# Weight sums for half of the up projection made in DRAM instead of on VectorE, in one paced list, with w_up laid out by blocks

## The chip, the cores and the metric

The kernel is one program on 1 core of one Trainium2 chip. The metric is the device time of one execution in microseconds, as the median of three runs. The profile is of one execution, read by a hardware profiler; its span is the time from the first to the last instruction that it shows.

## What is computed

One decoder layer on a sequence of 512 tokens of width 1024, in float32. An input projection feeds four token mixers of 4 heads each, their normed outputs go through one output projection, and a squared-ReLU MLP of width 4096 follows. The change touches the MLP and the weight loads around it:

```python
mixed = jnp.concatenate([rms_norm(gr, group_out_g[i]) for i, gr in enumerate(groups)], axis=-1)
x = x + mixed @ w_o
u = jax.nn.relu(rms_norm(x, mlp_norm_g) @ w_up)      # 1024 -> 4096
return x + (u * u) @ w_down                           # 4096 -> 1024
```

## The kernel before

**Split arithmetic.** TensorE works on fp32r operands. Each float32 operand is split into a rounded high part and a remainder, and a product is three matmuls, high x high, high x low, low x high (`mm3`). A weight block of 128x512 is loaded from DRAM into a raw room (tile `wraw`), ScalarE makes the high part (`whi<-wraw`), VectorE subtracts it to make the low part (`wlo<-wraw,whi`), and the pair waits in a pool of `WB` = 10 pairs until TensorE has used it.

**Fewer products.** Up and down projection use a Strassen-Winograd scheme: 7 products of half-size blocks in place of 8, paid for with sums of weight blocks and of activations. The up projection runs over 8 feature groups G of 512 columns and two halves c of the contraction. In a group, products 1, 2, 5, 6, 7, 3, 4 come in this order for c = 0 and then for c = 1; one product of one c is 12 matmuls of 128x256. Products 1, 2 and 4 use a raw block of weights. Products 5, 6, 7 and 3 use weight sums: VectorE makes them from the raw rooms, one `TENSOR_TENSOR` of 128x512 each, into tiles named `pT` and `sq` (`pair_load`, `split_st`): 4 sums for each (G, c), 64 in all. The accumulators of a group lie in banks named `ps_s`, `ps_o`, `ps_t` and `ps_acc`, two of each; `combine_first` and `combine` add them up on VectorE and ScalarE and so free them.

**Early products.** For the groups in `EARLY` = 1, 3, 5, 7, products 1 and 2 run ahead of group 0, during the norm of the residual stream (`first_products`). They need a bank of `ps_o` each.

**Rooms and loads.** There are three raw rooms of 128x1024. `pair_load` gets two of them for each (G, c) and fills each with one 512 KB transfer. The down projection uses the same rooms as six halves, plus `pT`, `pT`, `sq` once the up stage no longer needs them. Its own weight sums (products 5, 6, 7 for 8 pairs of blocks, 24 sums) are not made on VectorE: SyncE starts a DRAM-to-DRAM copy of 512 KB into a tile `wsum`, and GpSimd starts an accumulating DMA (`dma_add`) that adds the second block; `weight_sums(G)` ties each to the start of an attention unit or to the end of a product of the up stage.

**Order.** The program is written by a planner: generators for each piece of work (`pl.spawn(..., priority)`) are stepped against modelled engine clocks; `Get` and `pl.put` hand buffers round, `Wait` waits for named events. What it settles is only the order of instructions on each engine. On the chip each engine runs its list in order, and semaphores for data and buffers decide when. A transfer that waits for a room on SyncE therefore holds every later transfer of SyncE's list.

**Names in the profile.** `act` is L293, `tt` (a VectorE or GpSimd tensor_tensor) L301, `mm3`'s matmul L321, transposes L333, `dma` L338, `dma_add` L343. In the changed file the same helpers stand 11 lines further down.

## Time and profile before

| | us |
|---|---|
| median of 3 runs (606.76, 608.39, 612.29) | 608.39 |
| the profiled execution's own time | 607.45 |
| its span | 605.3 |

The profiled execution is 0.94 us under the median, and 2.15 us of its time lie outside the span. The up stage begins about 300 us after the span's start with group 0, the down projection's first matmuls are at about 450 us, and the last output is stored at the end of the span. A busy share is read with its stage: TensorE is busy in nearly all of the span, so time can be gained only where it waits or where its clock is low.

### The profile page before, as it was taken

To read this page: it belongs to the slowest core of one execution; us is meant where nothing else is said; L and a number is where in the kernel's file an instruction comes from. 1 tells how busy PE (TensorE), PEld (TensorE's weight loads), DVE (VectorE), ACT (ScalarE), POOL (GpSimd) and SP (SyncE) were. 2 spreads that over 40 slices of the span, in tenths; PEclk is the share of its full clock that TensorE was granted. 3 is DMA by queue.
4 is the path that set the end of the run, shared out by engine and by line. 5 is a ranking of instruction groups with operands and counts; after the bars stand their busy time and mean duration, and the time that the engine had idled before them with its cause. 6 is when DMAs were issued, how large, how long until landed. Compare 5 with 4: busy or idle time off the path is not lost.

```text
span 605.3 us, 10541 instructions
## 1 busy us (share of the span) xinstructions
PE 585.5 (97%) x3556; PEld 515.6 (85%) x3556; DVE 492.6 (81%) x1141; ACT 385.0 (64%) x877; POOL 102.3 (17%) x153
## 2 busy tenths in 40 slices
PE   8999998999999999999989999999979999999997
PEld 7978887887899878889989999999968888888885
DVE  4775669589978796669899999998989999989652
ACT  6766566467766675558657577566676766766640
POOL 5134453462312110000000000000011111100000
PEclk9999999999999999999989999999998999999999
DMA  6953905299986240404347767656598778656622
GB/s 196 291 161 93 317 10 140 43 196 309 322 141 106 35 140 1 140 11 130 105 139 201 197 180 198 189 184 182 142 301 218 188 192 200 169 179 220 192 85 104
DMA packets 54118, 99.06 MB, mean 164 GB/s; under 512 B 5238, under 2 KB 12976, under 8 KB 53936
## 3 DMA queue, kind: packets, MB, share of 16 engines
q1 hardware_dynamic: 44592, 81.42, 41.6%
q0 software_dynamic: 9312, 16.83, 17.1%
q8 instruction: 28, 0.46, 0.3%
q14 instruction: 26, 0.21, 0.1%
q10 hardware_dynamic: 160, 0.14, 0.1%
HBM read 96.27 MB, written 27.26 MB: 204 GB/s over the span
## 4 chain that ended last, share of the span: by engine, by line
PE 69%; DVE 13%; DMA 9%; ACT 5%; issue 3%; SPq 0%; DVEq 0%; ACTq 0%
PE ps_acc L321 21%; PE ps_o L321 17%; PE ps_t L321 14%; PE ps_s L321 13%; PE ps_t L333 4%; DMA wraw<-in_w_up_dram 3%; DMA wraw<-in_w_o_dram 3%; ACT whi L293 2%; DMA wraw<-in_w_in_dram 2%; DVE wlo L305 1%; DVE p L301 1%; DVE wlo L301 1%; DMA wraw<-wsum 1%; DVE q L305 1%; DMA rnb<-in_x_dram 1%
## 5 line engine op out<-in xcount | busy, mean ns | idle before, releaser
L321 PE MATMUL ps_acc<-whi,xT 128*128 128x512 f32 (+1 forms) x416 | 144.3, 403 | 0.8 <-ACT kT L293 0.4
L321 PEld LDWEIGHTS ps_acc<-whi,xT 128*128 128x128 f32 x416 | 77.7, 190 | 12.1 <-ACT kT L293 0.8
L321 PE MATMUL ps_acc<-wlo,xT 128*128 128x512 f32 (+1 forms) x208 | 83.3, 405 | 0.0
L293 ACT ACTIVATE whi<-wraw 128x512 fp32r<-128x512 f32 x95 | 59.0, 625 | 29.1 <-DMA wraw<-in_w_up_dram 6.6
L301 DVE TENSOR_TENSOR wlo<-wraw,whi 128x512 fp32r<-128x512 f32 x95 | 64.5, 686 | 10.7 <-ACT whi L293 10.4
L343 POOL DMA_DIRECT2D wsum<-in_w_down_dram x24 | 22.1, 1054 | 210.8 <-DMA wsum<-in_w_down_dram 209.2
L293 ACT ACTIVATE whi<-pT 128x512 fp32r<-128x512 f32 x57 | 35.7, 628 | 26.4 <-DVE pT L301 16.8
L293 ACT ACTIVATE p<-p,sm 128x256 f32<-128x256 f32 (+3 forms) x64 | 34.4, 539 | 18.1 <-DVE sm L1013 17.8
L321 PEld LDWEIGHTS ps_acc<-wlo,xT 128*128 128x128 f32 x208 | 39.6, 190 | 5.5
L321 PE MATMUL ps_s<-kT,q 128*128 128x256 f32 (+3 forms) x150 | 42.7, 334 | 1.5 <-DVE sm L1013 0.8
L301 DVE TENSOR_TENSOR wlo<-pT,whi 128x512 fp32r<-128x512 f32 x57 | 38.8, 686 | 3.4 <-ACT whi L293 3.3
L305 DVE SCALAR_TENSOR_TENSOR wlo<-wraw,ga_col,whi 128x512 fp32r<-128x512 f32 (+1 forms) x40 | 31.6, 803 | 10.4 <-ACT whi L293 10.1
L321 PE MATMUL ps_o<-kT,whi 128*128 128x256 f32 (+1 forms) x204 | 39.7, 289 | 0.0
L321 PEld LDWEIGHTS ps_o<-kT,whi 128*128 128x128 f32 x204 | 32.3, 190 | 0.6
L321 PEld LDWEIGHTS ps_s<-kT,q 128*128 128x128 f32 x150 | 26.8, 190 | 5.5 <-DVE sm L1013 2.4
L293 ACT ACTIVATE whi<-wraw,ga_col 128x512 fp32r<-128x512 f32 (+1 forms) x40 | 27.1, 700 | 5.0 <-DMA wraw<-in_w_in_dram 4.7
L321 PE MATMUL ps_o<-kT,wlo 128*128 128x256 f32 (+1 forms) x102 | 29.5, 290 | 0.6 <-DVE wlo L301 0.6
L321 PE MATMUL ps_o<-q,whi 128*128 128x256 f32 (+1 forms) x136 | 26.5, 292 | 2.6 <-ACT whi L293 2.5
L301 POOL TENSOR_TENSOR rnb<-rnb,sm 128x512 f32<-128x512 f32 (+3 forms) x20 | 18.0, 904 | 65.3 <-DVE sm L301 24.9
L333 PE MATMUL ps_t<-ident,p 128*128 128x128 f32 x148 | 26.7, 274 | 0.3 <-ACT p L293 0.3
L293 ACT ACTIVATE whi<-sq 128x512 fp32r<-128x512 f32 x28 | 17.5, 626 | 13.3 <-DVE sq L301 7.9
L321 PEld LDWEIGHTS ps_o<-q,whi 128*128 128x128 f32 x136 | 21.4, 191 | 3.5 <-issue 2.4
(542 smaller groups left out, 1736.8 us busy)
## 6 DMA issues: line engine op xcount, KB each, us to landing
wraw<-in_w_up_dram SPq DMA_DIRECT2D x32, 512.0 KB, 3.8
wsum<-in_w_down_dram POOLq DMA_DIRECT2D x24, 512.0 KB, 7.5
wraw<-wsum SPq DMA_DIRECT2D x36, 256.0 KB, 3.0
wsum<-in_w_down_dram SPq DMA_DIRECT2D x16, 512.0 KB, 6.7
wraw<-in_w_down_dram SPq DMA_DIRECT2D x32, 256.0 KB, 3.4
wraw<-in_w_in_dram SPq DMA_DIRECT2D x24, 256.0 KB, 3.1
wraw<-in_w_o_dram SPq DMA_DIRECT2D x16, 256.0 KB, 4.0
wsum<-wsum SPq DMA_DIRECT2D x8, 512.0 KB, 7.8
```

Of the source, the lines that this page charges most:

```text
L293: lambda: nc.scalar.activation(o, i, func, scale=scale, **kw), aps(o, accum), aps(i, scale, bias))
L301: lambda: E[eng].tensor_tensor(o, a, b, op=op), [o], [a, b])
L305: lambda: nc.vector.scalar_tensor_tensor(o, a, s, b, op0=op0, op1=op1), [o], aps(a, s, b))
L321: nc.tensor.matmul(o, l, r, start=first, stop=last)
L333: nc.tensor.transpose(o, i, ident[0:parts, 0:parts])
L343: return Op("pool", 1000.0 * nb / 262144, lambda: nc.gpsimd.dma_start(out=o, in_=i, accum_op=ALU.add), [o], [o], nb, 2100.0)
```

## The change

Five edits:

1. **Up sums in DRAM.** For groups 1, 3, 5 and 7 (`UPSUMS`) the four weight sums are made in DRAM (tiles `wsumu`), each by a copy on SyncE and an accumulating DMA on GpSimd, 16 of each. These groups then load five 256 KB blocks for each c, two to a room, in place of two 512 KB transfers. 32 VectorE sums go. Since a DMA only adds, the signs of three products are turned and three additions in `combine` become subtractions.
2. **One list of sums.** All 40 sums (16 up, then 24 down) stand in one list. Number n is released by the planner at 115,000 + 7,500 n ns of its TensorE clock, its add 8,000 ns later. On the chip this sets only the places of the copies in SyncE's list and of the adds in GpSimd's.
3. **Rows of the adds.** `dma_add` now cuts the rows of a transfer at 512 bytes (`max_dma_last_dim=512`; 128 elements), and the planner counts an add's bytes twice.
4. **w_up by blocks.** On the host, w_up is laid out so that each block of 128x512 is contiguous; the early loads read rows of 2 KB, not 1 KB.
5. **Rooms singly, four early banks.** `up_rooms` hands a room to the up stage as soon as both its halves are back, not all three at once; groups 3 and 7 take the `ps_acc` banks for their early products.

```diff
+UPSUMS = (1, 3, 5, 7)
+SUM_AT, SUM_NS, SUM_LAG = 115000.0, 7500.0, 8000.0
...
     def dma_add(o, i):
         nb = n_of(o) * o.shape[0] * 4
-        return Op("pool", 1000.0 * nb / 262144, lambda: nc.gpsimd.dma_start(out=o, in_=i, accum_op=ALU.add), [o], [o],
-                  nb, 2100.0)
+        return Op("pool", 1000.0 * nb / 262144, lambda: nc.gpsimd.dma_start(out=o, in_=i, accum_op=ALU.add,
+                                                                              max_dma_last_dim=512), [o], [o],
+                  2.0 * nb, 2100.0)
...
+    USUM = {(pr, G): dram.tile([2 * P, 512], F32, name=f"wsumu{pr}{G}", tag=f"wsumu{pr}{G}")
+            for G in UPSUMS for pr in (5, 6, 7, 3)}
...
-                k0 = (4 * j + 2 * c) * P
-                LOADS.append((("st", G, c, 1 + j), [(w_up[0, k0:k0 + 2 * P, G * 512:G * 512 + 256].rearrange(
-                    "(k p) f -> p k f", p=P), 512)], None, 1, None))
+                LOADS.append((("st", G, c, 1 + j), [(w_up[G, 0, j, c], 512)], None, 1, None))
...
             if q[0][0] == ("st", 0, 0):
-                for _ in range(2 * WRAW):
-                    yield Get("wraw")
-                for room in RAW2:
-                    pl.put("wraw2", room)
+                pl.spawn(up_rooms(), 1)
...
+        if G in UPSUMS:
+            srcs = {1: w_up[G, 0, 0, c], 2: w_up[G, 0, 1, c], 4: w_up[G, 1, 1, c]}
+            for j in range(0, len(todo), 2):
+                room = yield Get("wraw2")
+                left = [room, len(todo[j:j + 2])]
+                for n, pr in enumerate(todo[j:j + 2]):
+                    raw = room[:, n * 512:(n + 1) * 512]
+                    if pr not in srcs:
+                        yield Wait(("sum", pr, "up", G))
+                    yield dma(raw, srcs[pr] if pr in srcs else USUM[pr, G][c * P:(c + 1) * P])
+                    pl.spawn(split_sum(key(pr), raw, left, turn[pr]), split_prio)
+            return
...
+    def split_sum(key, raw, left, turn):
+        yield Wait(("turn", turn))
+        hi, lo = yield Get("w")
+        pl.events.add(("turn", turn + 1))
+        yield from split(hi, lo, raw)
+        left[1] -= 1
+        if not left[1]:
+            pl.put("wraw2", left[0])
...
     def first_products(G):
-        banks = {}
+        banks, tag = {}, ("o", "acc")[EARLY.index(G) % 2]
         for pr in (1, 2):
-            banks[pr] = yield Get("o")
+            banks[pr] = yield Get(tag)
...
-    def weight_sums(G):
-        for pr, ev, src in ((5, (G, 12 + G), rows(1, 1, G * 4, 2)), (6, (24 + 3 * G, 30 + 3 * G), rows(2, 2, G * 4 + 2, 2)),
-                            (7, (5, 3), rows(2, 2, G * 4 + 2, 2))):
...
+    def weight_sums():
+        for n, (where, pr, G, first, second) in enumerate(sum_list()):
+            dst = (USUM if where == "up" else WSUM)[pr, G]
+            yield At(SUM_AT + n * SUM_NS)
+            yield dma(dst, first)
+            pl.spawn(weight_add(SUM_AT + n * SUM_NS + SUM_LAG, where, pr, G, dst, second), 2)
+
+    def weight_add(at, where, pr, G, dst, src):
+        yield At(at)
+        yield dma_add(dst, src)
+        pl.events.add(("sum", pr, where, G))
```

TensorE's list is the same for the first 517 of some 2,720 entries, holds the same work in another order through the attention, and is the same again from group 0 of the up stage to the end. VectorE's list falls from 1118 to 1084 entries, SyncE's grows from 220 to 259, GpSimd's from 145 to 160.

VectorE at group 0, before. `pT` and `sq` hold weight sums of group 0, `whi` and `wlo` are split weights, and `xT<-ps_o_65` is `combine_first` of group 7, which frees the second bank of `ps_o`:

```order
L301 TENSOR_TENSOR pT_147<-wraw_107,sq_146 128x512
L301 TENSOR_TENSOR wlo_120<-sq_146,whi_119 128x512
L301 TENSOR_TENSOR wlo_126<-wraw_107,whi_125 128x512
L301 TENSOR_TENSOR wlo_124<-pT_147,whi_123 128x512
L301 TENSOR_TENSOR xT_2851<-ps_o_65,xT_2851 128x2x256
L301 TENSOR_TENSOR wlo_128<-wraw_108,whi_127 128x512
```

The same place in the changed kernel, where group 7's early products lie in the other pair of banks:

```order
L312 TENSOR_TENSOR pT_163<-wraw_122,sq_162 128x512
L312 TENSOR_TENSOR wlo_136<-sq_162,whi_135 128x512
L312 TENSOR_TENSOR xT_2870<-ps_acc_64,xT_2870 128x2x256
L312 TENSOR_TENSOR wlo_140<-pT_163,whi_139 128x512
L312 TENSOR_TENSOR wlo_144<-wraw_123,whi_143 128x512
L312 TENSOR_TENSOR pT_165<-wraw_123,wraw_124 128x512
```

The sums of group 0 stay where they were; the instruction that frees a bank now frees one of `ps_acc`, which group 0 needs only for its product 4, and product 6 finds its `ps_o` bank freed by group 5's early products.

VectorE at the end of the up stage, before: from `mixA` (the last combine of group 6) over the four sums and five splits of the last half of group 7 to the first block of the down projection, which is split into `kT`:

```order
L301 TENSOR_TENSOR mixA<-xT_2853,mixA 128x2x256
L301 TENSOR_TENSOR pT_147<-wraw_106,wraw_107 128x512
L301 TENSOR_TENSOR pT_149<-wraw_106 128x512
L301 TENSOR_TENSOR sq_146<-pT_147,wraw_106 128x512
L301 TENSOR_TENSOR wlo_124<-pT_147,whi_123 128x512
L301 TENSOR_TENSOR wlo_128<-pT_149,whi_127 128x512
L301 TENSOR_TENSOR pT_147<-wraw_107,sq_146 128x512
L301 TENSOR_TENSOR wlo_126<-sq_146,whi_125 128x512
L301 TENSOR_TENSOR wlo_112<-wraw_107,whi_111 128x512
L301 TENSOR_TENSOR wlo_110<-pT_147,whi_109 128x512
L301 TENSOR_TENSOR wlo_114<-wraw_108,whi_113 128x512
L301 TENSOR_TENSOR kT_2643<-wraw_106,kT_2643 128x512 x2
```

The same place in the changed kernel:

```order
L312 TENSOR_TENSOR wlo_140<-wraw_122,whi_139 128x512
L312 TENSOR_TENSOR mixA<-xT_2872,mixA 128x2x256
L312 TENSOR_TENSOR vB<-p_167,ps_acc_63 128x2x256
L312 TENSOR_TENSOR wlo_142<-wraw_122,whi_141 128x512
L312 TENSOR_TENSOR wlo_144<-wraw_123,whi_143 128x512
L312 TENSOR_TENSOR wlo_126<-wraw_123,whi_125 128x512
L312 TENSOR_TENSOR wlo_128<-wraw_124,whi_127 128x512
L312 TENSOR_TENSOR wlo_130<-wraw_122,whi_129 128x512
L312 TENSOR_TENSOR kT_2654<-wraw_123,kT_2654 128x512
```

The four sums are gone from the row, and the five splits read the rooms directly.

SyncE from the loads of group 7 to the first loads of the down projection, before (`wsum<-in_w_down` is the copy of a sum, `wraw<-wsum` the load of a finished one):

```order
L338 DMA wsum_94<-in_w_down_dram 256x512
L338 DMA wraw_107<-in_w_up_dram 128x2x512
L338 DMA wraw_108<-in_w_up_dram 128x2x512
L338 DMA wraw_106<-in_w_up_dram 128x2x512
L338 DMA wraw_107<-in_w_up_dram 128x2x512
L338 DMA wsum_95<-in_w_down_dram 256x512
L338 DMA wraw_108<-in_w_down_dram 128x512 x2
L338 DMA wraw_106<-wsum_73 128x512
L338 DMA wraw_106<-in_w_down_dram 128x512
L338 DMA wraw_107<-wsum_73 128x512
L338 DMA wraw_107<-in_w_down_dram 128x512
L338 DMA wsum_96<-in_w_down_dram 256x512
```

The second half of group 7 and the first down loads in the changed kernel:

```order
L349 DMA wraw_122<-wsumu_85 128x512
L349 DMA wraw_122<-wsumu_86 128x512
L349 DMA wraw_123<-wsumu_87 128x512
L349 DMA wsum_111<-in_w_down_dram 256x512
L349 DMA wraw_123<-wsumu_88 128x512
L349 DMA wraw_124<-in_w_up_dram 128x512
L349 DMA wsum_112<-in_w_down_dram 256x512
L349 DMA wraw_122<-in_w_down_dram 128x512 x2
L349 DMA wraw_123<-wsum_89 128x512
L349 DMA wraw_123<-in_w_down_dram 128x512
```

Between group 0's first loads and the first down loads SyncE's list had 7 copies and now has 18; among the first down loads it had one more and now has none.

## Rows read from the trace of the kernel before

**Rows 1.** The page: busy time, share of the span and instructions of each engine.

```profile
PE 585.5 (97%) x3556; PEld 515.6 (85%) x3556; DVE 492.6 (81%) x1141; ACT 385.0 (64%) x877; POOL 102.3 (17%) x153
```

**Rows 2.** Windows by stage: length; busy PE, PEld, DVE, ACT, POOL; clock, DMA share, GB/s.

```profile
105.00:240.00 135.00, 131.40 (x860) 113.62 (x861) 107.41 (x396) 90.04 (x295) 36.98 (x49) 1.00 0.61 145
240.00:300.00 60.00, 60.00 (x379) 53.78 (x378) 46.19 (x98) 38.68 (x83) 0.00 (x0) 1.00 0.31 97
300.00:315.00 15.00, 12.10 (x86) 11.58 (x85) 14.76 (x25) 8.71 (x16) 0.00 (x0) 0.89 0.44 127
315.00:435.00 120.00, 119.62 (x1010) 119.27 (x1009) 114.39 (x187) 78.92 (x139) 6.17 (x7) 1.00 0.66 182
435.00:465.00 30.00, 26.97 (x134) 22.39 (x133) 27.25 (x46) 20.91 (x39) 4.83 (x6) 0.94 0.90 261
465.00:600.00 135.00, 135.00 (x586) 109.79 (x586) 110.99 (x179) 79.58 (x134) 10.10 (x12) 1.00 0.60 166
```

**Rows 3.** Timeline of TensorE at group 0: start, duration, what, idle before.

```profile
301.59 0.48 PE L321 MATMUL ps_o<-kT,whi 128*128 128x256 f32 x2
302.70 0.38 PE L321 MATMUL ps_o<-kT,wlo 128*128 128x256 f32 x1 [0.64 <-DVE wlo L301]
...
303.51 0.28 PE L321 MATMUL ps_o<-kT,wlo 128*128 128x256 f32 x1
...
303.87 0.28 PE L321 MATMUL ps_o<-kT,wlo 128*128 128x256 f32 x1
306.41 0.47 PE L321 MATMUL ps_o<-q,whi 128*128 128x256 f32 x2 [2.26 <-ACT whi L293]
```

**Rows 4.** Timeline of VectorE at the same place.

```profile
301.96 1.29 DVE L301 TENSOR_TENSOR wlo<-pT,whi 128x512 fp32r<-128x512 f32 x2
...
303.77 0.68 DVE L301 TENSOR_TENSOR wlo<-sq,whi 128x512 fp32r<-128x512 f32 x1
...
305.58 0.68 DVE L301 TENSOR_TENSOR xT<-ps_o,xT 128x512 f32<-128x512 f32 x1
```

**Rows 5.** Windows of 5 us behind the two longest waits of TensorE.

```profile
306.00:311.00 5.00, 4.59 (x26) 4.62 (x27) 4.80 (x9) 3.75 (x7) 0.00 (x0) 0.66 0.49 125
453.00:458.00 5.00, 5.00 (x15) 4.00 (x16) 4.78 (x8) 3.39 (x6) 0.87 (x1) 0.66 1.03 259
```

**Rows 6.** Timeline of TensorE where the down projection begins.

```profile
448.79 0.40 PE L321 MATMUL ps_s<-q,wlo 128*128 128x512 f32 x1
451.73 0.73 PE L321 MATMUL ps_o<-q,tabC 128*128 128x512 f32 x2 [2.54 <-ACT tabC L293]
452.95 1.20 PE L321 MATMUL ps_o<-q,tabC 128*128 128x512 f32 x4 [0.49 <-DVE tabC L301]
```

**Rows 7.** Chain of waits ahead of it: start, duration, what.

```profile
430.24 1.21 DVE pT L301 x2
...
431.96 1.24 DVE wlo L301 x2
...
436.63 6.29 DMA wraw<-wsum
...
442.94 0.63 ACT q L293
```

**Rows 8.** Timeline of SyncE's transfers at the same place.

```profile
436.02 0.50 SPq L338 DMA_DIRECT2D wsum<-in_w_down_dram  x1
```

**Rows 9.** Timeline of TensorE in the attention stage, one of its waits.

```profile
148.84 0.45 PE L321 MATMUL ps_s<-kT,q 128*128 128x384 f32 x1 [0.44 <-DVE sm L1013]
```

**Rows 10.** DMA issues: count, KB each, median us from issue to landing.

```profile
wsum<-in_w_down_dram POOLq DMA_DIRECT2D x24, 512.0 KB, 7.5
wraw<-wsum SPq DMA_DIRECT2D x36, 256.0 KB, 3.0
```

**Rows 11.** Window of the crowded stretch ahead of the down projection.

```profile
435.00:450.00 15.00, 14.19 (x87) 12.40 (x85) 13.05 (x23) 10.40 (x20) 1.79 (x2) 1.00 0.90 285
```

More of the change, by code (lines that the diff above doesn't have):

```diff
@@ L230, in run @@
                         if q.key in self.events:
+                            self.step(p)
+                            moved = True
+                    elif type(q) is At:
+                        if self.clock["pe"] >= q.ns:
                             self.step(p)
@@ L544, in w_load @@
         for ap, w in pieces:
[L545 removed]
+            yield dma(raw[:, o:o + w], ap)
             o += w
@@ L595, in loads, with up_rooms @@
         yield from down_loads()
+    def up_rooms():
+        back = []
+        for _ in range(2 * WRAW):
+            back.append((yield Get("wraw")).tensor.name)
+            if back.count(back[-1]) == 2:
+                pl.put("wraw2", next(room for room in RAW2 if room.tensor.name == back[-1]))
     def down_rooms():
@@ L603, in pair_load @@
     def pair_load(G, c):
+        early = G in EARLY
+        key = lambda pr: ("st", G, c, pr)
+        todo = [pr for pr, _ in PRODUCTS if pr > 2 or not early]
+        turn = {pr: TURN["st", G, c] + n for n, pr in enumerate(todo)}
+        if G in UPSUMS:
[10 more added lines that the diff above has]
+            return
         rooms = []
@@ L606, in pair_load @@
             room = yield Get("wraw2")
-            k0 = (4 * j + 2 * c) * P
-            yield dma(halves(room), w_up[0, k0:k0 + 2 * P, G * 512:(G + 1) * 512].rearrange("(k p) f -> p k f", p=P))
+            yield dma(halves(room), w_up[G, :, j, c].rearrange("h p f -> p h f"))
             rooms.append(room)
-        (a11, a21), (a12, a22) = ([halves(room)[:, :, h * 256:(h + 1) * 256] for h in range(2)] for room in rooms)
-        early = G in EARLY
+        (a11, a21), (a12, a22) = ([room[:, h * 512:(h + 1) * 512] for h in range(2)] for room in rooms)
         left = {0: 4 - early, 1: 4 - early}
@@ L618, in done @@
                     pl.put("wraw2", rooms[j])
[L620 to L621 removed]
         S = {}
[L623 to L630 removed]
+        how = {1: (("raw", a11, 0), ()), 2: (("raw", a12, 1), ()), 5: (("sum", 1, a21, a22, (0, 1)), ()),
+               6: (("sum", 2, 1, a11, (0,)), (1,)), 7: (("sum", 3, a11, a21, (0,)), ()),
+               3: (("sum", 4, a12, 2, (1,)), (2,)), 4: (("raw", a22, 1), ())}
+        for pr in todo:
+            pl.spawn(split_st(key(pr), *how[pr], S, done, turn[pr], (G, c)), split_prio)
+    def split_sum(key, raw, left, turn):
[6 more added lines that the diff above has]
+            pl.put("wraw2", left[0])
+        W[key] = (hi, lo)
+        uses[key] = 1
+        pl.events.add(("W", key))
     def halves(ap):
@@ L646, in split_st @@
             tmp = yield Get("st")
-            v = halves(tmp)
+            v = tmp
             a, b = (S[z] if isinstance(z, int) else z for z in (a, b))
-            yield tt(v, a, b, op, "pool" if n in POOL_S else "dve")
+            yield tt(v, a, b, ALU.add)
             S[n] = v
@@ L653, in split_st @@
             dones = ()
-        yield from split(halves(hi), halves(lo), v)
+        yield from split(hi, lo, v)
         done(*dones)
@@ L1393, in block, with sum_list @@
         return rows(k, n, (s // 2) * 4 + (k - 1) * 2 + s % 2, 1)
-    def weight_sums(G):
-        for pr, ev, src in ((5, (G, 12 + G), rows(1, 1, G * 4, 2)), (6, (24 + 3 * G, 30 + 3 * G), rows(2, 2, G * 4 + 2, 2)),
-                            (7, (5, 3), rows(2, 2, G * 4 + 2, 2))):
-            yield Wait(("product", G, ev[0]) if pr == 7 else ("started", ev[0]))
-            yield dma(WSUM[pr, G], WSUM[5, G] if pr == 6 else rows(1, 2, G * 4, 2))
-            yield Wait(("product", G, ev[1]) if pr == 7 else ("started", ev[1]))
-            yield dma_add(WSUM[pr, G], src)
-            pl.events.add(("sum", pr, G))
+    def sum_list():
+        up, q = [], lambda G, h, j: w_up[G, h, j].rearrange("c p f -> (c p) f")
+        for a, b in zip(UPSUMS[0::2], UPSUMS[1::2]):
+            for G in (a, b):
+                up += [("up", 5, G, q(G, 1, 0), q(G, 1, 1)), ("up", 7, G, q(G, 0, 0), q(G, 1, 0))]
+            for pr, of, j in ((6, 5, 0), (3, 6, 1)):
+                up += [("up", pr, G, USUM[of, G], q(G, 0, j)) for G in (a, b)]
+        t1, t2, t3 = [], [], []
+        for G in range(DFF // 512):
+            b12, b22 = rows(1, 2, G * 4, 2), rows(2, 2, G * 4 + 2, 2)
+            t1.append(("down", 5, G, b12, rows(1, 1, G * 4, 2)))
+            t2.append(("down", 6, G, WSUM[5, G], b22))
+            t3.append(("down", 7, G, b12, b22))
+        mix = t1[0:2]
+        for G in range(DFF // 512):
+            mix += [t2[G]] + t1[G + 2:G + 3]
+        return up + mix + t3
+    def weight_sums():
[8 more added lines that the diff above has]
+        pl.events.add(("sum", pr, where, G))
     def down_loads():
@@ L1409, in down_loads @@
             if pr in (5, 6, 7):
-                yield Wait(("sum", pr, s // 2))
+                yield Wait(("sum", pr, "down", s // 2))
                 src = WSUM[pr, s // 2][(s % 2) * P:(s % 2 + 1) * P]
@@ L1609, in hybrid_kernel @@
     pl.spawn(sum_memory(), 200)
-    for G in range(DFF // 512):
-        pl.spawn(weight_sums(G), 2)
+    pl.spawn(weight_sums(), 2)
     pl.spawn(dense(), 2000)
```

31 lines of the change are left out of this document (12 added, 19 removed).

## The prediction

> **What bounds the kernel now.** I read the page first, then the busy time by stage, then the timeline and the chain of waits wherever TensorE stops. TensorE is busy for 585.5 us of a span of 605.3 [rows 1]. In three of the stages there is little or nothing to win from it: 240 to 300, 465 to 600 and all but 0.4 us of 315 to 435 are full at clock 1.00 [rows 2]. It loses time in three places. In the attention stage (105 to 240) it is idle 3.6 us in many small pieces. At 300 to 315 it is busy 12.10 of 15 us with a granted clock of 0.89, and at 435 to 465 it is busy 26.97 of 30 at 0.94 [rows 2]. The change keeps TensorE's work, so what it gains lies in these three places. VectorE is the runner-up: 114.39 of 120 us in the up stage.
>
> **Stop at group 0.** TensorE runs one product of 12 matmuls from 301.59, three matmuls in 0.36 us (303.51 to 303.87), so a product costs 1.43 us; then nothing starts before 306.41 [rows 3]. The view names a ScalarE split as the releaser, but the split it names would end after that start. By the code the matmuls at 306.41 are product 6 of group 0, which needs two things: its weights, whose low part VectorE has at 303.77 + 0.68 = 304.45, and the second bank of `ps_o`. That bank is freed by the sum `xT<-ps_o` of group 7, which stands behind the splits in VectorE's row and ends at 305.58 + 0.68 = 306.26 [rows 4]. The bank is the later one. After the wait TensorE's granted clock is 0.66 in the 5 us from 306 [rows 5], between its two levels of 1.2 and 2.4 GHz, which costs 5 x 0.34 = 1.7 us.
>
> The change puts the early products of groups 3 and 7 on `ps_acc`. Group 0 then finds its `ps_o` bank free, and it needs `ps_acc` only for product 4, three products (4.3 us) after product 6. What is late next is the low part of product 6: its third matmul needs it at 304.45, so the product may start near 304.2. The wait shrinks by 306.41 - 304.2 = 2.2 us. The idle of 0.64 us just before (302.70) was followed by matmuls at the full 0.12 us each [rows 3], so I count the low clock as gone too: 2.2 + 1.7 = 3.9. Against it, the last early splits stand one place later on VectorE, which can hold a load of group 0 back by up to one 0.60 us step (1.21 us for two, rows 7); I take 0.5. **Term: -3.4 us**, between -3.9 and 0. The 0.64 us of 302.70 stay, since they wait for a sum of group 0, which VectorE still makes.
>
> **Stop before the down projection.** After 448.79 the next matmul, due 0.23 us later, comes at 451.73, so 2.7 us are lost; 0.5 more at 452.95; and 5 us at clock 0.66 cost 1.7 [rows 5, 6]. Together 4.9. Followed back, the chain runs over ScalarE from 442.94, which waited for the transfer that took 6.29 us from 436.63 [rows 7], where the median for these blocks is 3.0 [rows 10]. SyncE had issued the 512 KB copy of a sum at 436.02, just ahead of it [rows 8]. Before that VectorE worked off sums and splits in one row of 0.60 us steps. The change takes the four sums of group 7's last half out of that row (4 x 0.60 = 2.4 us), and the copy out of the first down loads. Either the median landing (-3.3 us) or the shorter row nearly covers the 3.2 us of waiting; but two copies now stand just before these loads in SyncE's list and their adds run beside them, so I don't count all. **Term: -4.2**, between -4.9 and 0.
>
> **VectorE's 32 sums.** 32 x 0.60 = 19.2 us of VectorE go. TensorE is full in the up stage, so of itself this gives nothing beyond the 0.4 us of idle; it is the cover that lets VectorE keep ahead once TensorE comes 3.4 us earlier. Without it group 1 would start to wait.
>
> **Attention stage.** Sixteen copies that lay in 57 to 67 and 141 to 159 go, others come, and all engines' lists are shuffled. One wait of 0.44 us at 148.84 [rows 9] and its neighbour hang on loads of w_o behind those copies; that bounds the gain near 0.7. The bound on the other side is a second helping of the stage's own idle, 3.6 us. The list holds the same work and VectorE is only 80% busy here [rows 2], so I stay near the small gain. **Term: -0.4**, between -0.7 and +3.6.
>
> **Transfers in the up stage.** Groups 1, 3, 5 and 7 now load 5 blocks of 256 KB per half, 10.5 MB, the other four 8.4 MB. Between the loads of group 0 and the first down loads stand 18 sums, each a copy and an add of 0.52 MB, 18.9 MB. That is 37.8 MB in about 130 us, 290 GB/s, where before the stage moved 182 GB/s at a share of 0.66 [rows 2]. The nearest row with such a rate is 435 to 450, 285 GB/s at a share of 0.90 [rows 11], which is the stretch of the 6.29 us landing. So the engines can carry it, but loads may land late. Two things soften that: ten pairs of split weights are up to 14 us of TensorE work, and all eighteen sums are for the down projection, so that an add that comes late holds nobody yet. An add lands in 7.5 us [rows 10] and one comes every 7.2 us; the 512-byte rows have no row in the trace, so their price is only bounded, by nothing and by the slower case below. **Term: +1.0**, between 0 and +12.8. The 2 KB rows of the early loads, `up_rooms` and the host's layout I cost at nothing: the stage that they feed, 240 to 300, is full [rows 2].
>
> **Sum.** -3.4 - 4.2 - 0.4 + 1.0 = -7.0 against the profiled execution's 607.45: 600.45. That execution lies 0.94 under the median of 608.39, so on the scale of the medians **601.4 us**.
>
> **A rule that speaks against it.** The trace has transfers of SyncE and GpSimd in one share of 16 engines: 0.90 with copies, adds and loads together [rows 11]. The Trainium skill, page "DMA: Bandwidth & Descriptors", section "Issuing engines are not separate DMA queues", says that transfers run on the same 16 engines and interleave, whichever engine started them. By that rule a sum moved off VectorE isn't free but delays the loads of the very weights that it serves, which is the first rival; by the forecast the delay stays inside the cover. The trace agrees as far as the 6.29 us landing beside a copy goes.
>
> **Rivals.** *Rooms turn over too slowly (slower).* An early group's half needs three rooms in 5 x 1.43 = 7.1 us, so each of the three rooms must cycle in that. A cycle is an issue (0.5), the landing, two splits on ScalarE and the last one on VectorE (1.24 + 0.68 by the rows for VectorE's splits, rows 4 and 7): landing + 2.4. With the median landing of 3.0 it is 5.4 and fits; with 6.29 it is 8.7, and each of the 8 halves loses 1.6, 12.8 us in all: 600.45 + 12.8 + 0.94 = 614.2, slower than before. It decides from a landing of 4.7 us on. For it speaks the rate of 290 GB/s; against it that the median landing held at 0.66 and that sums can lag.
>
> *The attention stage gives back 3.6 us.* 600.45 + 0.4 + 3.6 + 0.94 = 605.4. For it: GpSimd's norm products stand in one list with the adds, and an add that waits for its copy holds them; against it: GpSimd is busy only 36.98 of 135 us there [rows 2].
>
> *One stop stays (the change does not do what it says).* At group 0, if the split that the view names was the true releaser, or before the down projection, if its rooms come free only when the third room of group 7 is split: 601.4 + 3.4 = 604.8, or 601.4 + 4.2 = 605.6.
>
> **How the numbers follow.** About 1% (6.1 us) is what a measurement of this kernel can tell from no change: under 602.3 is faster, over 614.5 slower. Chances: the forecast 0.45, slow rooms 0.21 (0.10 of it at milder landings, which end between the two bounds, 0.11 beyond them), attention 0.12, one stop staying 0.22. Faster gets the forecast alone, 0.45; slower 0.11; the rest, 0.44, lies within 1%. All terms at their good ends give 607.45 - 3.9 - 4.9 - 0.7 + 0.94 = 598.8, and the runs shown reach 1.6 us below their median, so the range begins at 597.0. It ends at 612.0, which takes in both middle rivals and the milder slow rooms.
>
> **What the profile after would show.** Right: between product 5 and 6 of group 0 a wait under 0.5 us and clock 1.00 behind it; at the start of the down projection no wait over 1 us; VectorE's busy time near 492.6 - 32 x 0.69 = 470; a DMA share near 0.9 from 315 to 435 with landings of `wraw` at 3 to 4.5 us. Wrong: waits of TensorE for splits whose releaser is a `wraw` transfer, at each of groups 1, 3, 5 and 7 (slow rooms); more than 4 us of idle TensorE in 105 to 240 (attention); a low clock in one of the two old places.

## The result, and the profile after

The changed kernel takes 613.09 us (median of 15 runs, 610.62 to 615.59) beside 607.9 for the kernel before (15 runs); the ratio is 1.0077, with a 95% interval of 1.0048 to 1.0106. It is slower by 0.8%, some 5 us, where 601.4 and a gain had been forecast and 612.0 was the end of the range. The profiled execution has a span of 611.3 us, 6.0 more than before.

The page and the windows by stage, after (columns as in rows 2):

```profile
PE 585.9 (96%) x3556; PEld 516.2 (84%) x3556; DVE 471.2 (77%) x1106; ACT 384.1 (63%) x879; POOL 152.3 (25%) x169
```

```profile
105.00:240.00 135.00, 131.98 (x869) 115.48 (x869) 106.80 (x400) 92.91 (x301) 42.84 (x48) 1.00 0.76 160
240.00:300.00 60.00, 56.88 (x343) 50.70 (x342) 44.24 (x92) 35.40 (x77) 13.15 (x8) 0.97 1.00 215
300.00:315.00 15.00, 14.89 (x123) 14.52 (x122) 13.91 (x23) 9.66 (x18) 3.52 (x2) 1.00 0.86 225
315.00:435.00 120.00, 116.83 (x979) 115.89 (x978) 97.08 (x157) 76.58 (x139) 27.13 (x16) 1.00 1.12 272
435.00:465.00 30.00, 25.38 (x139) 21.37 (x138) 21.90 (x36) 18.68 (x35) 4.86 (x4) 0.94 0.98 230
465.00:600.00 135.00, 134.20 (x580) 108.53 (x579) 114.53 (x185) 83.34 (x141) 16.71 (x13) 1.00 0.69 177
```

TensorE's busy time is what it was [rows 1], so its work did not grow. VectorE lost 21.4 us, about the 22 that 32 sums of 0.69 make. The stop at group 0 is gone: TensorE is busy for 14.89 of 15 us from 300 to 315, at clock 1.00 [rows 2]. The window 105 to 240 gained 0.6 us of TensorE. But 240 to 300 lost 3.1, 315 to 435 lost 2.8 and 435 to 465 lost 1.6. The DMA share went from 0.31 to 1.00 in the first of these three and from 0.66 to 1.12 in the second. (The share adds up the time that packets took, so it can pass 1.00.)

Windows at fixed times cut the work at different places. From group 0 on TensorE's list is the same in both kernels, so its first matmul of group 0 and its first of the down projection can be compared, before and then after:

```profile
298.53 0.40 PE L321 MATMUL ps_s<-kT,whi 128*128 128x256 f32 x2
...
440.82 0.39 PE L321 MATMUL ps_s<-whi,whi 128*128 128x512 f32 x1
```

```profile
302.27 0.40 PE L332 MATMUL ps_s<-kT,whi 128*128 128x256 f32 x2
...
443.71 0.39 PE L332 MATMUL ps_s<-whi,whi 128*128 128x512 f32 x1
```

Group 0 begins 3.7 us later. The up stage takes 141.4 us in place of 142.3. From the first matmul of the down projection, which comes at 441 and 444 us and not at about 450, to the end of the span it is 167.6 us in place of 164.5. These three make the 6.0 us.

The DMA issues after (count, KB each, median us to landing) and the clock behind two of the stops shown below (the last columns are clock, DMA share, GB/s):

```profile
wsum<-in_w_down_dram POOLq DMA_DIRECT2D x24, 512.0 KB, 10.1
wraw<-wsum SPq DMA_DIRECT2D x36, 256.0 KB, 3.4
...
wraw<-in_w_up_dram SPq DMA_DIRECT2D x16, 512.0 KB, 5.4
wraw<-wsumu SPq DMA_DIRECT2D x32, 256.0 KB, 6.0
```

```profile
277.00:282.00 5.00, 2.13 (x12) 2.13 (x13) 3.30 (x10) 2.65 (x7) 1.75 (x1) 0.82 1.12 307
451.00:456.00 5.00, 4.71 (x15) 3.80 (x15) 5.00 (x10) 4.73 (x9) 1.32 (x1) 0.67 0.65 222
```

An add of a sum lands in 10.1 us, where it took 7.5 [rows 10]. The loads of the up sums, which lie in the up stage, land in 6.0, against 3.4 for the same size of load in the down projection. The timeline of TensorE at its three longest stops, and a piece of the chain of waits behind each:

```profile
279.87 0.83 PE L344 MATMUL ps_t<-ident,pT 128*128 128x128 f32 x4 [3.12 <-DVE pT L316]
...
430.88 0.47 PE L332 MATMUL ps_o<-q,whi 128*128 128x256 f32 x2 [2.00 <-ACT whi L304]
...
451.29 1.22 PE L332 MATMUL ps_o<-kT,whi 128*128 128x512 f32 x2 [4.01 <-DVE xT L312]
```

```profile
270.58 7.13 DMA wraw<-in_w_up_dram
...
416.52 6.00 DMA wraw<-wsumu
...
435.34 7.56 DMA wraw<-wsum
```

The idle times are 3.12, 2.00 and 4.01 us, and the clock is 0.82 and 0.67 in the windows of 5 us at the first and the third of them. Each chain leads back to a load of raw weights that landed 6.0 to 7.6 us after it was free to go: an early load of w_up, a finished up sum, a finished down sum. The third stop stands in the place of the one of rows 6 and 7, but is not the same: it comes 21 matmuls earlier in TensorE's list, and at the old place 0.61 us of waiting are left of 2.54 and 0.49.

The late block itself is not what TensorE lacked at these stops. VectorE works through its list in order. The split of the late block stood at the head of that list, and what TensorE needed stood behind it. Here are, for each stop, that split (with VectorE's idle time before it) and the instruction that TensorE waited for:

```profile
278.46 0.69 DVE L312 TENSOR_TENSOR wlo<-wraw,whi 128x512 fp32r<-128x512 f32 x1 [3.34 <-ACT whi L304]
279.07 0.75 DVE L316 SCALAR_TENSOR_TENSOR pT<-kBl,sm,vB 128x512 f32<-128x512 f32 x1
...
423.26 0.69 DVE L312 TENSOR_TENSOR wlo<-wraw,whi 128x512 fp32r<-128x512 f32 x1 [2.00 <-ACT whi L304]
430.05 0.68 DVE L312 TENSOR_TENSOR vB<-ps_o,p 128x512 f32<-128x512 f32 x1
...
443.58 0.69 DVE L312 TENSOR_TENSOR kT<-wraw,kT 128x512 fp32r<-128x512 f32 x1 [5.53 <-ACT kT L304]
450.55 0.68 DVE L312 TENSOR_TENSOR xT<-ps_o,p 128x512 f32<-128x512 f32 x1
```

The first is a piece of the norm, ready at 279.82. The other two are sums of `combine` that by the code free a bank of `ps_o`; they end at 430.73 and 451.23, and TensorE goes on at 430.88 and 451.29. This is the kind of wait that held group 0 before the change [rows 4]. For the second stop the view names a ScalarE split; for the same stop in e10_actcopy it names the sum `vB`. That these two stops wait for the bank is read from the code and the times; no run moved these banks.

### The profile page after: what moved, and what is told of

It is laid out like the page before. It is cut to its first block, busy times and chain, and to the rows that moved or that the text cites. A ratio compares the mean times of both kernels' runs of the same rounds, so it can differ in the third digit from the quotient of the medians.

```text
span 611.3 us, 10598 instructions
## 1 busy us (share of the span) xinstructions
PE 585.9 (96%) x3556; PEld 516.2 (84%) x3556; DVE 471.2 (77%) x1106; ACT 384.1 (63%) x879; POOL 152.3 (25%) x169
## 4 chain that ended last, share of the span: by engine, by line
PE 58%; DMA 16%; DVE 13%; ACT 6%; issue 5%; SPq 0%; POOL 0%; DVEq 0%; ACTq 0%; POOLq 0%
PE ps_acc L332 20%; PE ps_o L332 13%; PE ps_s L332 12%; PE ps_t L332 9%; DMA wraw<-in_w_up_dram 5%; PE ps_t L344 5%; DMA wraw<-wsumu 4%; DVE wlo L312 3%; ACT whi L304 2%; DMA wraw<-wsum 2%; DVE wlo L316 2%; DMA wraw<-in_w_in_dram 1%; DMA wraw<-in_w_down_dram 1%; DVE p L312 1%; DMA rnb<-in_x_dram 1%
## 5 line engine op out<-in xcount | busy, mean ns | idle before, releaser
L304 ACT ACTIVATE whi<-wraw 128x512 fp32r<-128x512 f32 x127 | 77.9, 624 | 55.5 <-DMA wraw<-in_w_up_dram 16.8
L312 DVE TENSOR_TENSOR wlo<-wraw,whi 128x512 fp32r<-128x512 f32 x127 | 85.9, 687 | 31.4 <-ACT whi L304 31.2
L354 POOL DMA_DIRECT2D wsum<-in_w_down_dram x24 | 42.2, 1758 | 149.8 <-DMA wsum<-in_w_down_dram 93.7
L332 PE MATMUL ps_o<-kT,whi 128*128 128x256 f32 (+1 forms) x172 | 34.6, 295 | 4.7 <-DVE xT L312 4.0
L332 PEld LDWEIGHTS ps_o<-kT,whi 128*128 128x128 f32 x172 | 27.3, 192 | 6.1 <-DVE xT L312 4.4
L354 POOL DMA_DIRECT2D wraw<-in_w_down_dram x11 | 14.2, 1290 | 61.4 <-DVE wlo L312 44.3
L312 POOL TENSOR_TENSOR sq<-rnb 128x384 f32<-128x384 f32 (+1 forms) x16 | 18.5, 1157 | 41.4 <-ACT rnb L304 36.6
L304 ACT ACTIVATE whi<-pT 128x512 fp32r<-128x512 f32 x36 | 22.5, 627 | 9.8 <-DVE pT L312 4.6
L312 DVE TENSOR_TENSOR wlo<-pT,whi 128x512 fp32r<-128x512 f32 x36 | 24.4, 685 | 2.8 <-ACT whi L304 2.7
L332 PE MATMUL ps_o<-kT,wlo 128*128 128x256 f32 (+1 forms) x86 | 25.3, 295 | 0.4 <-DVE wlo L312 0.4
## 6 DMA issues: line engine op xcount, KB each, us to landing
wsum<-in_w_down_dram POOLq DMA_DIRECT2D x24, 512.0 KB, 10.1
```

Source lines behind the costliest of these rows:

```text
L304: lambda: nc.scalar.activation(o, i, func, scale=scale, **kw), aps(o, accum), aps(i, scale, bias))
L312: lambda: E[eng].tensor_tensor(o, a, b, op=op), [o], [a, b])
L332: nc.tensor.matmul(o, l, r, start=first, stop=last)
L354: return Op("pool", 1000.0 * nb / 262144, lambda: nc.gpsimd.dma_start(out=o, in_=i, accum_op=ALU.add, max_dma_last_dim=512), [o], [o], 2.0 ...
```

## The experiments

All were run against the kernel before; the ratio stands with its interval. The letters: A, the engines are full with the sums' transfers and loads land late (A1 the down sums in the up stage, A2 of these the adds); B, copies that wait for an add hold SyncE's list; C, the new order, the layout or the rooms cost the time; D, five loads a half through three rooms are too slow by themselves; E, copies ahead of the loads in SyncE's own queue.

**Rows of the adds (e1_rows).**

```diff
-                                                                              max_dma_last_dim=512), [o], [o],
+                                                                              max_dma_last_dim=2048), [o], [o],
```

> The changed kernel with the adds in rows of 2 KB in place of 512 bytes; every engine's order stays as in the change. Theory A (the 16 DMA engines are full from 240 us on, and loads of raw weights land late): the adds' share of the engines falls from 34.0% towards 25% (40 sums at the price that 24 had before), the share from 315 to 435 falls from 1.12 to about 1.0, the 256 KB loads of finished sums land in 4 to 5 us instead of 6.0, and 2 to 4 us come back: ratio to the kernel before 1.002 to 1.005. Theory B (copies that wait for an add hold SyncE's list, so that loads are issued late): the order is the same, nothing comes back, ratio 1.007 to 1.009. A third outcome, slower than the change, would say that short rows let the loads through between the adds.

613.26 us, ratio 1.0086 (1.0055 to 1.0117): as slow as the change. A window and an issue row of it:

```profile
315.00:435.00 120.00, 113.92 (x943) 113.16 (x942) 95.33 (x153) 74.25 (x133) 14.10 (x16) 0.99 0.97 269
```

```profile
wraw<-wsumu SPq DMA_DIRECT2D x32, 256.0 KB, 6.0
```

The row of the page on the accumulating queue (packets, MB, share of 16 engines), in the change and here:

```profile
q0 software_dynamic: 50528, 25.22, 34.0%
```

```profile
q0 software_dynamic: 13664, 25.22, 25.4%
```

The share from 315 to 435 fell from 1.12 to 0.97, as expected, but the landing stayed at 6.0, and the stops only moved. So it isn't the engine time that the short rows add. It missed theory A's numbers and could not decide for B.

**Four early banks alone (e2_banks).** The kernel before, and in `first_products`:

```diff
-        banks = {}
+        banks, tag = {}, ("o", "acc")[EARLY.index(G) % 2]
...
-            banks[pr] = yield Get("o")
+            banks[pr] = yield Get(tag)
...
-                pl.spawn(combine_first(G, banks, {1: "o", 2: "o"}), 20)
+                pl.spawn(combine_first(G, banks, {1: tag, 2: tag}), 20)
```

> The kernel before with one part of the change alone: the early products of groups 3 and 7 in the other pair of banks. If the bank was what product 6 of group 0 waited for, the wait of 2.3 us there and the low clock behind it go, 3.4 to 4.4 us: ratio 0.993 to 0.995. If the split that the view names was the releaser, the wait stays and the ratio is 1.000. The waits before the down projection stay at some 4.9 us by every theory.

603.16 us, ratio 0.9918 (0.9886 to 0.9950), a little beyond the good end of what was expected, which its interval takes in. Two windows:

```profile
300.00:315.00 15.00, 14.24 (x118) 13.83 (x117) 14.85 (x25) 10.49 (x19) 0.00 (x0) 1.00 0.44 143
...
435.00:465.00 30.00, 27.56 (x112) 21.71 (x111) 26.23 (x43) 20.48 (x36) 5.29 (x6) 0.89 0.91 249
```

Against 12.10 us and clock 0.89 [rows 2], the first is nearly full at clock 1.00. The bank was the releaser. In the second the old stop is still there. The same two matmuls as above:

```profile
298.30 0.40 PE L321 MATMUL ps_s<-kT,whi 128*128 128x256 f32 x2
...
436.07 0.39 PE L321 MATMUL ps_s<-whi,whi 128*128 128x512 f32 x1
```

The up stage takes 137.8 us here, 4.5 less than before.

**No up sums in DRAM (e3_noup).**

```diff
-UPSUMS = (1, 3, 5, 7)
+UPSUMS = ()
```

> The changed kernel without sums of the up projection in DRAM: VectorE makes all 64 again, the list holds the 24 sums of the down projection alone and so ends before the up stage. Theories A and B: the new waits of TensorE at 276, 428 and the longer one at 447 go, since the sums' transfers leave the up stage; what is left is the gain at group 0 and the old wait before the down projection: ratio 0.990 to 0.996. Theory C (the shuffled order, the host's layout or the rooms handed on singly cost the time): ratio stays above 1.004.

600.32 us, ratio 0.9881 (0.9837 to 0.9924), a little beyond the good end of what was expected. Two windows and an issue row:

```profile
315.00:435.00 120.00, 119.16 (x1004) 118.64 (x1003) 116.75 (x192) 80.87 (x142) 0.00 (x0) 1.00 0.42 130
435.00:465.00 30.00, 30.00 (x144) 25.01 (x144) 28.52 (x48) 23.03 (x43) 6.45 (x5) 1.00 0.84 220
```

```profile
wraw<-in_w_up_dram SPq DMA_DIRECT2D x32, 512.0 KB, 3.5
```

C falls: with TensorE's order, layout, rooms and short rows as in the change, the kernel is faster. With the list 16 sums shorter no sum starts beyond 315 us, the share from there to 435 is 0.42. The stop at the start of the down projection, which was expected to stay, is gone (30.00 of 30 us at clock 1.00), although VectorE makes all 64 sums.

**Waiting copies on GpSimd (e4_poolcopy).**

```diff
-            yield dma(dst, first)
+            yield (dma_pool if first.tensor.name.startswith("wsum") else dma)(dst, first)
```

> The changed kernel with the copies that start from another sum (those that must wait until that sum's add has landed) issued by GpSimd in place of SyncE. The bytes stay the same. Theory A: loads land as late as before, ratio 1.005 to 1.010. Theory B: SyncE's list is free of those waits, loads are issued up to some us earlier, and most of the 6 us come back: ratio 1.000 to 1.003.

618.53 us, ratio 1.0172 (1.0128 to 1.0216): slower still, outside what either theory gave. Its loads of up sums land as late, in 5.9 us. That speaks against B, but GpSimd's list became longer too, so a cleaner test follows (e13).

**The second four** separate the place of the down sums from the five-block loads.

```diff
-        return up + mix + t3
+        return up
...
-            if pr in (5, 6, 7):
-                yield Wait(("sum", pr, "down", s // 2))
-                src = WSUM[pr, s // 2][(s % 2) * P:(s % 2 + 1) * P]
```

> The changed kernel without the 24 sums of the down projection: products 5, 6 and 7 of the down projection read a raw block of weights of the same size instead (the sums are left out of the computation). The up sums in DRAM, their loads in five blocks and their three rooms stay. Theory A1 (the down sums, which now fall into the up stage, fill the engines there and delay the loads): with those 18 sums gone the share from 315 to 435 falls to about 0.45, loads land in 3 to 4 us, the new waits go, ratio 0.985 to 0.992. Theory D (five loads a half through three rooms are too slow by themselves): waits at groups 1, 3, 5 and 7 stay, ratio above 1.000.

```diff
-SUM_AT, SUM_NS, SUM_LAG = 115000.0, 7500.0, 8000.0
+SUM_AT, SUM_NS, SUM_LAG = 95000.0, 5000.0, 8000.0
```

> The changed kernel with its 40 sums paced from 95 us in steps of 5.0 us in place of 115 and 7.5, so that the last starts before the up stage. Nothing is left out. Theory A1: the up stage is free of sums, its waits go, and VectorE and the loads keep ahead; ratio 0.985 to 0.995, less what the fuller attention stage gives back (up to 3 us). Theory D: the waits at groups 1, 3, 5 and 7 stay, ratio above 1.000.

```diff
-UPSUMS = (1, 3, 5, 7)
-SUM_AT, SUM_NS, SUM_LAG = 115000.0, 7500.0, 8000.0
+UPSUMS = ()
+SUM_AT, SUM_NS, SUM_LAG = 235000.0, 7500.0, 8000.0
```

> The kernel with no up sums in DRAM (VectorE makes all 64), but with the 24 down sums paced as in the change, from 235 us in steps of 7.5, so that 18 of them lie in the up stage. Theory A1: loads land late again, in 5 us or more, and some of the waits come back, although no group loads five blocks: ratio 1.000 to 1.010. Theory D: nothing happens in the up stage, ratio 0.988 to 0.994, at most the old wait before the down projection comes back.

```diff
-UPSUMS = (1, 3, 5, 7)
+UPSUMS = ()
...
-                                                                              max_dma_last_dim=512), [o], [o],
+                                                                              max_dma_last_dim=2048), [o], [o],
```

> The kernel with no up sums in DRAM and the down sums ahead of the up stage (ratio 0.988 when it ran), with the adds in rows of 2 KB in place of 512 bytes; the orders are the same. If the adds' engine time counts in the stretch from 240 to 300, where the share was 1.01, 1 to 2 us come back: ratio 0.985 to 0.988; if not, the same time.

*e5_nodown*: 596.56 us, ratio 0.9818 (0.9783 to 0.9852), below what A1 gave. The five-block loads alone are no burden: TensorE is full in the up stage and those loads land in 2.7 us.

```profile
315.00:435.00 120.00, 120.00 (x1006) 119.64 (x1005) 100.56 (x162) 81.73 (x142) 0.00 (x0) 1.00 0.46 146
```

```profile
wraw<-wsumu SPq DMA_DIRECT2D x32, 256.0 KB, 2.7
```

*e7_late*: 617.06 us, ratio 1.0151 (1.0114 to 1.0187), above what A1 gave. No group loads five blocks, and yet the 512 KB loads of w_up land in 6.0 us (3.5 without sums in the stage) and TensorE loses 11 us of 120:

```profile
315.00:435.00 120.00, 108.93 (x867) 107.40 (x866) 100.18 (x166) 68.10 (x121) 24.57 (x14) 0.94 0.98 230
```

```profile
wraw<-in_w_up_dram SPq DMA_DIRECT2D x32, 512.0 KB, 6.0
```

The two together decide for A1 and against D. e7_late says one thing more: its down sums are paced as in the change, and the change, with 32 sums fewer on VectorE, is the faster of the two (1.0077 against 1.0151, intervals apart). Where loads land late, a shorter row of VectorE does help.

*e6_early*: 620.27 us, ratio 1.0212 (1.0173 to 1.0250), far from the expected gain. In this order three of the 40 sums copy another sum ahead of its add and so lack a block, against what the expectation says; the transfers are all there. Three windows:

```profile
105.00:240.00 135.00, 127.49 (x829) 110.33 (x829) 103.58 (x382) 87.26 (x279) 55.47 (x56) 1.00 1.07 221
240.00:300.00 60.00, 58.57 (x361) 51.37 (x359) 45.51 (x109) 37.03 (x89) 23.26 (x14) 1.00 1.19 266
300.00:315.00 15.00, 9.08 (x62) 8.26 (x62) 9.42 (x16) 8.16 (x16) 5.26 (x3) 0.94 1.22 282
```

Here the crowd stands in 105 to 315, at shares of 1.07 to 1.22, and TensorE loses 7.5, 1.4 and 5.9 us there. It doesn't end there either: the four adds started from 300 to 317 land after 30.4 us in the median, so the up stage was not free of sums, and TensorE loses another 4.4 us from 315 to 435. At this pace 40 sums did not fit ahead of the up stage.

*e8_noup2k*: 603.67 us, ratio 0.9912 (0.9874 to 0.9950). The 1 to 2 us that were hoped for did not come. Its runs spread from 597.2 to 606.2 and its interval overlaps that of e3_noup, so the row size changes nothing that these runs can tell.

**The last five** ask what of the down sums delays the loads, and how far the good part goes.

```diff
-        yield dma_add(dst, src)
+        if where == "up":
+            yield dma_add(dst, src)
```

> The changed kernel without the 24 adds of the down sums (each of those sums is then a copy of its first block alone, so the sums are left out of the computation); all copies stay where they are in SyncE's list, the up sums are whole. What of the down sums delays the loads? Theory A2 (the adds, which take most of the engines' time): with them gone from the up stage loads land in 3 to 4 us and the time falls to that without down sums, ratio 0.982 to 0.990. Theory E (the copies, which stand ahead of the loads in SyncE's own queue): loads still land in 5 to 6 us, ratio 1.000 to 1.006. The copies that wait for an add go out earlier in this kernel, since there is no add to wait for.

```diff
-            yield dma(dst, first)
+            yield dma(dst, first, "act" if where == "down" and first.tensor.name.startswith("in_") else "sp")
```

> The changed kernel with the 16 copies of down sums that read w_down issued by ScalarE, so that they lie in a queue other than the loads'; bytes, adds and the other copies stay. Theory A2: loads land as late as in the change, ratio 1.005 to 1.012 (and a little more, as ScalarE's list has 16 more entries). Theory E: the loads are free of most copies, land in 4 us, ratio 0.995 to 1.002.

```diff
-            t2.append(("down", 6, G, WSUM[5, G], b22))
+            t2.append(("down", 6, G, b12, b22))
```

> The changed kernel with the eight copies of down sum 6 made from the raw block in w_down in place of sum 5, so that no copy of a down sum in SyncE's list waits for an add (sum 6 then lacks one block, which is left out of the computation). The number of transfers, their bytes and all 24 adds stay. Theory A2 (the adds in flight delay the loads, whatever the order): loads of finished up sums still land in 5 to 6 us, ratio 1.002 to 1.010. Theory B (the waits in SyncE's list make the loads late): with them gone the time falls as far as it did without adds, ratio 0.980 to 0.992.

*e9_noadd*: 597.91 us, ratio 0.9815 (0.9775 to 0.9855), the same as without any down sum, with all copies still made by SyncE. *e10_actcopy*: 616.54 us, ratio 1.0125 (1.0081 to 1.0168). *e13_nochain*: 613.59 us, ratio 1.0088 (1.0054 to 1.0123). The issue rows of the up sums' loads in the three, in this order, and the up stage of the first:

```profile
wraw<-wsumu SPq DMA_DIRECT2D x32, 256.0 KB, 3.0
```

```profile
wraw<-wsumu SPq DMA_DIRECT2D x32, 256.0 KB, 5.8
```

```profile
wraw<-wsumu SPq DMA_DIRECT2D x32, 256.0 KB, 6.4
```

```profile
315.00:435.00 120.00, 116.56 (x980) 116.00 (x979) 97.55 (x157) 78.71 (x137) 0.00 (x0) 1.00 0.60 202
```

E falls: with 16 of the 24 copies in another engine's queue the loads are as late as they were (5.8 us), and with all copies but no adds they are not late (3.0). B falls: with no copy of a down sum waiting for an add, the loads land in 6.4 us and the time stays that of the change. What is left is A2, the adds in flight beside the loads: without them the loads land in 3.0 us.

That is a median, and TensorE is busy for only 116.56 of 120 us in the profiled execution of e9_noadd, the longest of its six. Where copies and loads bunch up, loads are late there too, with no add under way; a window, and the four loads of up sums issued between 309.2 and 312 us:

```profile
310.00:315.00 5.00, 5.00 (x45) 5.00 (x44) 3.09 (x5) 1.97 (x4) 0.00 (x0) 1.00 0.84 298
```

```profile
wraw<-wsumu SPq DMA_DIRECT2D x4, 256.0 KB, 6.2
```

TensorE then stops for 1.62 us at 320.10. So a stretch near 300 GB/s makes loads late even without adds, and with the adds the change moves 272 GB/s through the whole stage, where it is 202 here. The two matmuls of group 0 and of the down projection in this run:

```profile
296.93 0.40 PE L332 MATMUL ps_s<-kT,whi 128*128 128x256 f32 x2
...
437.64 0.39 PE L332 MATMUL ps_s<-whi,whi 128*128 128x512 f32 x1
```

Against the change, group 0 begins 5.3 us earlier, the up stage is 0.7 us shorter, and the rest, to the end of its span of 598.5, 6.7 us shorter.

```diff
-UPSUMS = (1, 3, 5, 7)
-SUM_AT, SUM_NS, SUM_LAG = 115000.0, 7500.0, 8000.0
+UPSUMS = ()
+SUM_AT, SUM_NS, SUM_LAG = 115000.0, 6500.0, 8000.0
```

> The kernel with no up sums in DRAM (ratio 0.988), its 24 down sums paced in steps of 6.5 us in place of 7.5, so that the last starts at 264 us and none runs at 285 to 315. If what it still loses at group 0 (1.1 us) and in 240 to 300 (0.9 us) comes from the last sums, 1 to 2 us come back: ratio 0.984 to 0.988. If not, the same time.

```diff
-UPSUMS = (1, 3, 5, 7)
-SUM_AT, SUM_NS, SUM_LAG = 115000.0, 7500.0, 8000.0
+UPSUMS = (5, 7)
+SUM_AT, SUM_NS, SUM_LAG = 110000.0, 5700.0, 6000.0
```

> The changed kernel with up sums in DRAM for groups 5 and 7 alone, and all 32 sums paced from 110 us in steps of 5.7 (the add 6.0 us later), so that none starts in the up stage; every sum is whole. By theory A1 the up stage is free of sums and VectorE is relieved of 16 of them where it was tightest, so the wait before the down projection and those of the up stage are gone: ratio 0.982 to 0.990. If the stretch from 105 to 300 can't carry 32 sums beside w_o and the early loads, waits come back there as with 40 sums in steps of 5.0: ratio 0.995 to 1.010.

*e11_noup65*: 595.02 us, ratio 0.9774 (0.9739 to 0.9810), the fastest whole kernel of the study, 2.3% ahead of the kernel before. It is better than expected: of the 3.2 us between its profiled execution and that of e3_noup (spans of 594.1 and 597.3) 1.2 lie in 300 to 315, where the expectation put them, and the rest is not settled. Three windows:

```profile
300.00:315.00 15.00, 15.00 (x129) 15.00 (x128) 15.00 (x26) 9.49 (x18) 0.00 (x0) 1.00 0.56 176
315.00:435.00 120.00, 119.45 (x1007) 119.20 (x1006) 115.79 (x191) 81.51 (x143) 0.00 (x0) 1.00 0.40 128
435.00:465.00 30.00, 30.00 (x132) 24.44 (x131) 28.67 (x48) 22.17 (x42) 7.74 (x6) 1.00 0.87 210
```

Group 0 (300 to 315) and the start of the down projection are full at clock 1.00.

*e12_up57*: 605.70 us, ratio 0.9954 (0.9925 to 0.9984), at the worse of the two outcomes. Its up stage is free of sums and nearly full (119.01 of 120 us), but the crowd has moved ahead of it:

```profile
240.00:300.00 60.00, 57.40 (x348) 51.22 (x347) 44.21 (x90) 36.03 (x79) 17.59 (x10) 0.97 1.17 247
```

Eight more sums than in e11_noup65, at a denser pace, cost 1.8%, and the VectorE time that they free (16 ops of 0.69 us) is worth less than that.

## Why the prediction was wrong, step by step

**The step that failed** is the price of the sums' transfers to the loads beside them: +1.0 in the up stage (between 0 and +12.8), nothing for the early loads ahead of it, and a gain of 4.2 at the start of the down projection that took a landing near the median of 3.0 us for granted. The working had the right row in hand, 285 GB/s and the 6.29 us landing [rows 7, 11], and computed 290 GB/s; the stage then moved 272 at a share of 1.12, and loads landed in 6.0. By stage, in the profiled executions, against the 13.0 us by which the forecast missed:

- *Ahead of group 0*: 3.7 us later, where -0.4 had been forecast and the early loads had been costed at nothing. Sums 16 to 21 brought the share there from 0.31 to 1.00, and an early load landed in 7.13 us.
- *Up stage*: 0.9 us shorter, where -3.4 and +1.0 made -2.4. The banks alone gave 4.5 (e2_banks), so the transfers cost 3.6 here, not 1.0.
- *From the down projection's first matmul on*: 3.1 us longer, where -4.2 had been forecast. This is the largest miss, 7.3 us.

Taking away the adds of the down sums brings the ratio from 1.0077 to 0.9815: they cost 2.6%, about 16 us of 608, over all stages together. How the loss splits over the stages differs from run to run of the same traffic: in e1_rows the stop ahead of group 0 is 0.52 us, not 3.12, and the up stage takes 146.8 us, not 141.4.

**Why the reasons for a small price did not hold.** That an add that comes late holds nobody fits e13_nochain, where taking away the copies that wait for adds changed nothing; but the loads beside an add are late while it is under way. The ten pairs of split weights did cover much: TensorE waited for no more than 0.45 us at a time from group 0 to 428 us. What they do not cover is VectorE's list. A late load leaves VectorE idle at that block's split, and the sums behind it free their banks late; the working had met just this at group 0 and did not ask where else it could happen.

**A nearer row.** The working hangs the waits near 148.84 [rows 9] on loads of w_o. One of those loads:

```profile
135.56 12.92 DMA wraw<-in_w_o_dram
```

From 135 to 150 us the kernel before moved 284 GB/s at a share of 1.09, with sums under way. So a landing of 12.92 us stood there to be read, twice the worst that was taken into account.

**Group 0 (-3.4).** Right. In the change and in e2_banks the wait between products 5 and 6 and the low clock behind it are gone; alone it is worth 0.8% (0.5 to 1.1), 4 to 5 us with the good end expected at 3.9. The releaser that the view named was indeed not the true one, though the reading alone was thin: the split that it named ended with the start of the matmul (305.78 + 0.63 us), not after it.

**Before the down projection (-4.2).** That the stop depends on the landing of its first blocks was right, the sign of the outcome was not: 6.29 us before, 7.56 in the change, where the longest stop is 4.01 us. Where no sum runs ahead of it (e3_noup, e11_noup65) it is gone altogether. Taking VectorE's sums out of the row was not needed for that: e3_noup makes them all. The rival that one stop stays had this place in view, but only with the stop as long as before.

**VectorE's 32 sums at nothing.** Right where loads land in time: the fastest whole kernel makes all 64 sums on VectorE, which is busy for 115.79 of 120 us in its up stage, with TensorE at 119.45. So they were not needed as a cover either. Where loads land late they are worth something, as the change against e7_late shows.

**Attention stage (-0.4).** TensorE's idle time there fell by 0.6, within the bounds.

**The slow rival** had the right sign and the right landing, but not the right mechanism, and that its 614.2 lies so near 613.09 is luck. It had rooms turn over too slowly under five loads a half, 1.6 us lost in each of 8 halves of the up stage. e5_nodown shows these loads landing in 2.7 us with TensorE full, e7_late shows losses with two loads a half, and the change lost most of its time outside the up stage. With a chance of 0.21, of which 0.11 lay beyond 614.5, it had been given too little.

**A sum.** The terms at their good ends make 598.9, not 598.8; nothing hangs on it.

**The rule that spoke against it.** The Trainium skill, page "DMA: Bandwidth & Descriptors", section "Issuing engines are not separate DMA queues", which stood against the change, was borne out: 16 copies moved to ScalarE's queue left the loads' landing at 5.8 us. The same page of the Trainium skill, section "Why small descriptors are slow (HBM only)", gives about 3 cycles of overhead for each packet beside one cycle for 32 bytes; an estimate from that is 76 cycles for four rows of 512 bytes against 67 for one of 2 KB, 13% more. Here the accumulating queue took 34.0% of the 16 engines' span with short rows and 25.4% with long ones for the same bytes, a third more, so the measurement goes beyond the page's figure, which is not given for accumulating transfers. In the time it did not show.

**What stays open** is how an add delays a load. With rows of 2 KB the share was 0.97 and the loads were as late as with short rows at 1.12, so the share alone doesn't set the landing. Whether the delay arises in the engines' queues or at the memory that both use, and whether plain transfers of the same bytes would delay the loads as much as the adds do, no run here tells. e13_nochain and e10_actcopy keep the whole traffic; a run with half the adds' bytes at the same count was not made.

## What to carry to other kernels

Work moved from a busy engine to DMA is paid by the loads beside it: compute the rate of the stage with the new transfers, look for a stretch of the trace that already runs at that rate, and take its landing time as the new one, before counting on buffers to cover it. Ask too what stands behind the late block in the list of the engine that splits it: a sum that frees a bank there stops TensorE even when split weights are in store. A chain of sums in DRAM belongs where few loads run, and a longer list pushes its tail out of there: here the 16 added sums moved 18 others into the up stage. When several edits come as one change, run the parts alone: without the up sums, and with a tighter pace, the other edits ran 2.3% faster than before; with the up sums, and the down sums that they pushed on, all of that was lost and more.

## What the runs showed of the hardware that was not expected

A third more traffic doubled the landing of plain loads, when that third was accumulating DRAM-to-DRAM transfers. Copies alone at 202 GB/s in the up stage left the loads at 3.0 us (share 0.60); copies with adds, 272 GB/s, made it 6.0, and it stayed there when longer rows brought the adds' queue from 34.0% to 25.4%. That adds weigh more than plain transfers of the same bytes is not shown. The short rows also cost GpSimd: an add of 512 KB occupied it for 1.75 us against 0.88 before.
